# Both output projections in half blocks, the last gate group projected after the queries, and two steps a call beside the last gate block of layer one

## The chip, the core and the metric

The kernel runs on one core of a Trainium2 chip. The core has five engines with queues of their own: TensorE (PE: matmuls and transposes; PEld is its weight load), VectorE (DVE), ScalarE (ACT), GpSimd (POOL) and SyncE (SP, which here only issues transfers). Each engine works through its own list of instructions in order; between engines they wait for each other by semaphores. Matmuls write to PSUM, everything else lives in SBUF, and weights come from HBM by DMA. The metric is the time on the device in microseconds (us) of one execution; lower is better.

## The reference

Two layers over 256 tokens of width 2048, 16 heads of 128. Layer one is a gated delta rule with short convolutions, layer two is softmax attention over a band of chunks (with 256 tokens, all earlier chunks lie in it). Each has one combined input projection, a SiLU gate z that multiplies the branch, and an output projection that is added to the residual.

```python
def gated_deltanet(h, w_in, conv_w, a_log, dt_bias, out_norm_w, w_out):
    proj = h @ w_in                       # q, k, v (2048 each), z (2048), a, b (16 each)
    qkv = silu(causal_depthwise_conv(qkv, conv_w))
    ...                                   # l2-normed q, k; chunked delta rule, state between chunks
    o = rms_norm(o, out_norm_w) * silu(z)
    return o @ w_out

def chunk_band_attention(h, w_in, q_norm_w, k_norm_w, rel_bias, w_out):
    proj = h @ w_in                       # q, k, v, z (2048 each)
    q, k = rms_norm(q, q_norm_w), rms_norm(k, k_norm_w)
    ...                                   # softmax(q k / sqrt(128) + bias) @ v per head
    o = o * silu(z)
    return o @ w_out

for i in range(2):
    hn = rms_norm(h, norm_w[i])
    h = h + (gated_deltanet if i == 0 else chunk_band_attention)(hn, ...)
```

## The kernel before

**The matmuls.** All data and weights are float32. For the projections each operand is split into a high part (float32r, a cast on ACT, L195) and the rest (a subtraction on DVE, L196), and three products are summed: high x high, high x low, low x high. Weights come in chunks of 512 KB by SP, 320 of them, listed in `plan`; a chunk is two blocks of 128 input rows by 512 columns, or four by 256. Of the raw chunk there are four buffers, of each split part three, and `fetch` runs three chunks ahead (`LOOK`). So the cast and the subtraction of a chunk wait until the matmuls of an earlier chunk have let go of a buffer.

**Three forms of a projection block.** In each, one *set* of products is 128 output features x 128 input rows x 256 tokens.
- `features` (L225): 512 columns; per set three matmuls of 256 columns each (L228, L230, L231).
- `half` (L233): 256 columns; the high and the low part of the data lie side by side, so the weight's high part takes both in one matmul of 512 columns (L238), and its low part follows with one of 256 (L241): two matmuls per set. The result stands in two halves, and ACT copies one out (L304 `ev`, or L873) before DVE adds them (L305).
- `tokens` (L244): tokens on the partitions, three matmuls of 512 columns (L247 to L249).

A block accumulates over all 16 input tiles `kt` in one of two PSUM buffers `psp`; the small products of the mixers use four buffers `pss`.

**The background.** All that is not projection (convolution, delta rule, norms, attention) is written as Python generators that stand in two lists, `bgq` and `bg2`. After each pair or group of matmuls `chunk` calls `step(rate)`, which advances one generator by one piece, `rate` times. `drain()` runs everything that is left. A scheduler then orders each engine's instructions anew from data dependences, free buffers and this order as priority; the order that it leaves is the one that the engines run.

**Where the two layers end.** The output projection contracts over the heads: input tile `kt` is head `kt`'s gated output, in `gmem["h"]` and `gmem["l"]`. `ready(gmem)` steps the background until head `kt` is there. The last four heads come late, since their chain begins with the last input block. So each projection opens two blocks at once: first `kt` 0 to 11 of both (`CUT` = 6 of 8 chunks each), then `drain()`, then `kt` 12 to 15 of both. Before, those two are `features` blocks of 512 columns; four `half` blocks of 256 follow.

**The chain of the last four heads in layer one**, by lines: `v_small` transposes v on PE (L744), scales it on DVE (L746), multiplies by the inverse on PE (L753, ACT copy L755), corrects the second half on PE and DVE (L760, L763), multiplies again (L753, L755); `v_back` forms the outputs on PE (L776 to L778), squares on ACT (L779), sums on DVE (L785, L786), takes the power on POOL (L788), scales (L794); `za_small(3)` multiplies by the gate z (L710); `gated` transposes on PE (L814) and splits on ACT and DVE (L818, L819). Then `ha_small` adds the residual, which POOL's queue loads (L869), and splits it for layer two.

**The end of layer two.** For each group of four heads: keys, queries, `qk_norm`, and `attend` in four stages per head: `scores` (L1010, L1011, then DVE and exponentials on ACT, L1023), `weights` (L1031), `turned` (three transposes L1037, ACT copy L1039 `pT`), `values` (L1047, L1048). At the end of `values` DVE multiplies by the gate (L1050), ACT and DVE split (L1051, L1052). The gates z come first in layer two (four groups of 512 columns, `zb_small`: L320 scales, L935 SiLU on ACT). The tiles `ev` and `pT` share two buffers.

## Time and profile before

| what | value |
|---|---|
| time, median of 3 runs | 1024.39 us (1023.38 to 2028.42) |
| profiled execution, its own time | 1024.26 us |
| profiled execution, span first to last instruction | 1022.4 us |
| PE busy / PEld busy | 1007.9 us (99%) / 881.1 us (86%) |
| DVE busy / ACT busy / POOL busy | 694.8 us (68%) / 520.2 us (51%) / 76.3 us (7%) |
| mean granted TensorE clock | 0.997 |
| DMA | 177.55 MB, 174 GB/s |

The profiled execution takes 1.86 us more than its span, and is 0.13 us below the median. A row of the timeline gives the start and the length in us, the engine, line, operation, the tiles and shapes, how many instructions were merged, and in brackets the idle time before it with what ended it. A group of lines has the count, busy us and mean ns. Matmuls overlap, so two that follow each other are compared by their starts.

### The profile page before, as it was taken

Reading aid. Unit: us, or ns where it says so; the run is one execution under the profiler, and the core shown is the slowest. Engines: PE = TensorE matmul, PEld = TensorE weight load, DVE = VectorE, ACT = ScalarE, POOL = GpSimd, SP = SyncE. Lnnn points to the kernel's source line nnn. Section 1 sums busy time; section 2 is a strip of 40 time slices with the busy share of each in tenths; the row PEclk is TensorE's granted clock in tenths of the full one; section 3 lists DMA queues with packets and bytes.
Section 4 is the critical chain, followed back from the end, with each engine's and each line's share of the span. In section 5 each row is a group of like instructions: output and inputs, shape, how many; then the busy total and the mean of one; then the engine's idle time right before and its main releaser. Section 6 shows DMA issues by size and latency. Waiting matters only on the chain.

```text
span 1022.4 us, 15569 instructions
## 1 busy us (share of the span) xinstructions
PE 1007.9 (99%) x6094; PEld 881.1 (86%) x6094; DVE 694.8 (68%) x1111; ACT 520.2 (51%) x720; POOL 76.3 (7%) x91
## 2 busy tenths in 40 slices
PE   8999999999999999999999999999999999999998
PEld 7988788888788989899988888888888888889987
DVE  6699879998799587755766555444456666656553
ACT  7465756453646555544654444444445555555442
POOL 1004000112000000001000000000011010101000
PEclk9999999999999999999999999999999999999999
DMA  8655566555576355545856766666665555554572
GB/s 292 177 147 144 162 175 180 143 164 158 157 199 165 105 145 145 158 151 157 255 186 183 228 207 205 190 194 195 188 188 176 148 178 151 167 163 146 174 227 72
DMA packets 133736, 177.55 MB, mean 174 GB/s; under 512 B 7584, under 2 KB 89632, under 8 KB 133664
## 3 DMA queue, kind: packets, MB, share of 16 engines
q1 hardware_dynamic: 132512, 172.38, 57.1%
q0 software_dynamic: 1152, 4.19, 1.2%
q8 instruction: 47, 0.77, 0.3%
q14 instruction: 25, 0.20, 0.1%
HBM read 174.46 MB, written 2.10 MB: 173 GB/s over the span
## 4 chain that ended last, share of the span: by engine, by line
PE 95%; DVE 2%; ACT 1%; DMA 1%; issue 1%; SPq 0%; DVEq 0%; ACTq 0%
PE psp L238 27%; PE psp L241 14%; PE psp L248 11%; PE psp L249 11%; PE psp L247 11%; PE psp L231 4%; PE psp L228 4%; PE psp L230 4%; PE pss L556 2%; PE pss L753 1%; PE pss L992 1%; PE pss L1011 1%; PE pss L1047 1%; DMA wt<-in_a_w_in_dram 1%; DVE wlo L196 1%; PE pss L1037 1%
## 5 line engine op out<-in xcount | busy, mean ns | idle before, releaser
L196 DVE TENSOR_TENSOR wlo<-wt,whi 128x1024 fp32r<-128x1024 f32 (+1 forms) x321 | 392.9, 1226 | 247.2 <-ACT whi L195 238.8
L195 ACT CAST whi<-wt 128x1024 fp32r<-128x1024 f32 (+1 forms) x321 | 336.7, 1050 | 410.9 <-PE psp L238 164.0
L238 PE MATMUL psp<-xb,whi 128*128 128x512 f32 x960 | 265.7, 396 | 3.6 <-DVE ev L305 2.0
L248 PE MATMUL psp<-wlo,xb 128*128 128x512 f32 x512 | 201.1, 393 | 1.6 <-DVE wlo L196 1.6
L249 PE MATMUL psp<-whi,xb 128*128 128x512 f32 x512 | 201.5, 393 | 0.0
L247 PE MATMUL psp<-whi,xb 128*128 128x512 f32 x512 | 200.0, 391 | 0.0
L238 PEld LDWEIGHTS psp<-xb,whi 128*128 128x128 f32 x960 | 165.0, 190 | 25.9 <-DVE ev L305 2.2
L241 PEld LDWEIGHTS psp<-xb,wlo 128*128 128x128 f32 x960 | 148.4, 189 | 20.1
L241 PE MATMUL psp<-xb,wlo 128*128 128x256 f32 x960 | 157.6, 283 | 0.0
L248 PEld LDWEIGHTS psp<-wlo,xb 128*128 128x128 f32 x512 | 96.1, 188 | 21.7 <-DVE wlo L196 2.0
L247 PEld LDWEIGHTS psp<-whi,xb 128*128 128x128 f32 x512 | 96.2, 188 | 20.1 <-ACT whi L195 0.3
L249 PEld LDWEIGHTS psp<-whi,xb 128*128 128x128 f32 x512 | 96.2, 188 | 19.1
L228 PE MATMUL psp<-g,whi 128*128 128x256 f32 x256 | 73.4, 287 | 0.0
L230 PE MATMUL psp<-g,whi 128*128 128x256 f32 x256 | 73.3, 287 | 0.0
L231 PE MATMUL psp<-g,wlo 128*128 128x256 f32 x256 | 72.7, 284 | 0.0
L238 PE MATMUL psp<-g,whi 128*128 128x512 f32 x248 | 67.7, 394 | 0.0
L499 DVE SCALAR_TENSOR_TENSOR cv<-raw,sm,cv 128x254 f32<-128x254 f32 (+2 forms) x144 | 61.8, 474 | 0.1
L230 PEld LDWEIGHTS psp<-g,whi 128*128 128x128 f32 x256 | 49.1, 192 | 0.2
L228 PEld LDWEIGHTS psp<-g,whi 128*128 128x128 f32 x256 | 49.1, 192 | 0.1
L231 PEld LDWEIGHTS psp<-g,wlo 128*128 128x128 f32 x256 | 49.1, 192 | 0.1
L238 PEld LDWEIGHTS psp<-g,whi 128*128 128x128 f32 x248 | 42.4, 189 | 5.7
L241 PEld LDWEIGHTS psp<-g,wlo 128*128 128x128 f32 x248 | 38.1, 189 | 5.3
(239 smaller groups left out, 980.1 us busy)
## 6 DMA issues: line engine op xcount, KB each, us to landing
wt<-in_b_w_in_dram SPq DMA_DIRECT2D x128, 512.0 KB, 3.7
wt<-in_a_w_in_dram SPq DMA_DIRECT2D x127, 512.0 KB, 3.9
wt<-in_a_w_out_dram SPq DMA_DIRECT2D x32, 512.0 KB, 4.5
wt<-in_b_w_out_dram SPq DMA_DIRECT2D x32, 512.0 KB, 4.0
g<-in_xT_dram SPq DMA_DIRECT2D x8, 256.0 KB, 4.5
dl<-in_xT_dram POOLq DMA_DIRECT2D x4, 512.0 KB, 5.4
dl<-in_relb_dram POOLq DMA_DIRECT2D x4, 512.0 KB, 5.2
out_dram<-cv SPq DMA_DIRECT2D x2, 512.0 KB, 4.2
```

The costliest lines, as they stand in the source:

```text
L195: act.copy(out=hi[:, js], in_=wt[:, js])
L196: dve.tensor_tensor(out=lo[:, js], in0=wt[:, js], in1=hi[:, js].bitcast(F32), op=ALU.subtract)
L228: pe.matmul(ps, lhsT=hi[:, j, fs], rhs=xb[:, kt, 0, :], start=(kt == 0 and s % 2 == 0), stop=False, skip_group_check=True)
L230: pe.matmul(ps, lhsT=hi[:, j, fs], rhs=xb[:, kt, 1, :], start=False, stop=False, skip_group_check=True)
L231: pe.matmul(ps, lhsT=lo[:, j, fs], rhs=xb[:, kt, 0, :], start=False, stop=(kt == KT - 1), skip_group_check=True)
L238: pe.matmul(ps[:, s], lhsT=hi[:, j, s * P:(s + 1) * P], rhs=xb[:, ks[j], :, :], start=(ks[j] == 0), stop=False, skip_group_check=True)
L241: pe.matmul(ps[:, s, 0, :], lhsT=lo[:, j, s * P:(s + 1) * P], rhs=xb[:, ks[j], 0, :], start=False, stop=(ks[j] == KT - 1), skip_group_chec ...
L247: pe.matmul(ps, lhsT=xh, rhs=hi[:, j, :], start=(kt == 0), stop=False)
L248: pe.matmul(ps, lhsT=xh, rhs=lo[:, j, :], start=False, stop=False)
L249: pe.matmul(ps, lhsT=xl, rhs=hi[:, j, :], start=False, stop=(kt == KT - 1))
L499: dve.scalar_tensor_tensor(out=cv[:, i, s:], in0=raw[:, i, :T - s], scalar=conv_w(i0 + i, 3 - s), in1=cv[:, i, s:], op0=ALU.mult, op1=ALU.add)
L556: pe.matmul(dst, lhsT=kq[:, a, i, c:c + P], rhs=rhs, start=(n == 0), stop=(n == 2))
```

## The change

- **Both output projections are made of eight `half` blocks.** The two blocks that are opened together have 256 columns each, not 512, and are cut after `CUTH` = 3 of 4 chunks, again at `kt` 12. `ha_small` always copies `ev` on ACT first; the outputs go out in pieces of two feature tiles (`out_half`), and `out_small` is gone.
- **The last gate group of layer two** (columns 7680 to 8191 of `b_w_in`) is projected after the last queries, just ahead of the output projection. `values` of the last four heads therefore leaves the ungated result in `late` (an ACT copy), and `late_gates` multiplies and splits it once the gates are there, two heads at a time. The load of the last group of biases hangs on the first group of v in place of the last gate group.
- **`rate` is 2** in the last gate block of layer one.

```diff
-    CUT = (3 * CPB) // 4
     CUTH = (3 * CPH) // 4
-    def cut_halves(w, col):
+    def cut_halves(w, col, n=6):
...
-        return p + halves(w, col + 512, 6)
-    for c0, c1 in ((0, CUT), (CUT, CPB)):
-        for j in range(2):
-            plan += wide(a_w_out, 512 * j, c0, c1)
-    plan += halves(a_w_out, 1024, 4)
-    plan += cut_halves(b_w_in, 6144)
+        return p + halves(w, col + 512, n)
+    plan += cut_halves(a_w_out, 0)
+    plan += cut_halves(b_w_in, 6144, 4)
...
-    for c0, c1 in ((0, CUT), (CUT, CPB)):
-        for j in range(2):
-            plan += wide(b_w_out, 512 * j, c0, c1)
-    plan += halves(b_w_out, 1024, 4)
+    plan += halves(b_w_in, 7680, 2)
+    plan += cut_halves(b_w_out, 0)
...
-    bgq.append(za_small(3, block("tokens", xb)))
+    bgq.append(za_small(3, block("tokens", xb, 2)))
...
-    def ha_small(n, ps, ks):
+    def ha_small(ps, ks):
...
-        two = len(ps.shape) == 4
-        if two:
-            ev = work.tile([P, 2, T], F32, name="ev", tag="ev")
-            act.copy(out=ev, in_=ps[:, :, 1, :])
+        ev = work.tile([P, 2, T], F32, name="ev", tag="ev")
+        act.copy(out=ev, in_=ps[:, :, 1, :])
         yield 1
-        if n < 2:
-            dve.tensor_copy(out=hmem["h"][0:1, k0 + 8, 0:1], in_=ps[0:1, 0, 0:1])
-        dve.tensor_tensor(out=h, in0=ps[:, :, 0, :] if two else ps, in1=h, op=ALU.add)
-        if two:
-            dve.tensor_tensor(out=h, in0=h, in1=ev, op=ALU.add)
+        if k0 in (0, 4):
+            dve.tensor_copy(out=hmem["h"][0:1, k0 + 8, 0:1], in_=ev[0:1, 0, 0:1])
+        dve.tensor_tensor(out=h, in0=ps[:, :, 0, :], in1=h, op=ALU.add)
+        dve.tensor_tensor(out=h, in0=h, in1=ev, op=ALU.add)
...
-    pa = [acc("features") for _ in range(2)]
-    for n in (CUT, CPB - CUT):
+    pa = [acc("half") for _ in range(2)]
+    for n in (CUTH, CPH - CUTH):
         for j in range(2):
-            if n != CUT and j == 0:
+            if n != CUTH and j == 0:
                 drain()
             for _ in range(n):
-                chunk("features", pa[j], gmem["b"], 2, ready(gmem))
-            if n != CUT:
-                a_done(j, pa[j], 4 * j, 4 * j + 4)
-    for j in range(4):
-        a_done(j + 2, block("half", gmem["b"], 2), 8 + 2 * j, 10 + 2 * j)
+                chunk("half", pa[j], gmem["b"], 2, ready(gmem))
+            if n != CUTH:
+                bgq.append(ha_small(pa[j], slice(2 * j, 2 * j + 2)))
+    for j in range(2, 8):
+        bgq.append(ha_small(block("half", gmem["b"], 2), slice(2 * j, 2 * j + 2)))
...
-    for j in (1, 2, 3):
+    for j in (1, 2):
         bgq.append(zb_small(j, pair(xb)))
...
+            if gi == 3:
+                act.copy(out=late[:, i, :], in_=ps[:, :T])
+                return
...
+    late = hmem["m"][:, 8192:9216].rearrange("p (h t) -> p h t", h=4)
+    def late_gates():
+        for i in range(0, 4, 2):
+            o, hs = late[:, i:i + 2, :], slice(12 + i, 14 + i)
+            dve.tensor_tensor(out=o, in0=o, in1=bmem["z"][:, hs, :], op=ALU.mult)
+            act.copy(out=gmem["h"][:, hs, :], in_=o)
+            dve.tensor_tensor(out=gmem["l"][:, hs, :], in0=o, in1=gmem["h"][:, hs, :].bitcast(F32), op=ALU.subtract)
+            gmem["done"] = 14 + i
+            yield 1
...
+    bgq.append(zb_small(3, pair(xb)))
+    bgq.append(late_gates())
...
-    po = [acc("features") for _ in range(2)]
+    po, evs = [acc("half") for _ in range(2)], [[], []]
...
-    for n in range(4, 7):
+    for n in range(2, 7):
```

The built programs show what stands where. Up to the first row of layer one's output projection TensorE's list is the same in both. Line numbers of the changed kernel differ: there L190 and L191 are the cast and the subtraction (L195, L196 before), L233 and L236 the two matmuls of a `half` set (L238, L241), L299 and L300 the two halves of an eviction (L304, L305).

First TensorE in layer one, where the outputs of the last four heads are formed. Before, L776 to L778 are those products, and L228 to L231 the matmuls of the projection:

```order
L776 MATMUL pss<-dl 128x128
L777 MATMUL pss<-dl 128x128
L778 MATMUL pss<-dl 128x128
L230 MATMUL psp<-g,whi 128x256
L231 MATMUL psp<-g,wlo 128x256
L228 MATMUL psp<-g,whi 128x256
```

Now the same products are L771 to L773, and L809 (L814 before) are the transposes of the gated heads:

```order
L771 MATMUL pss<-dl 128x128
L772 MATMUL pss<-dl 128x128
L773 MATMUL pss<-dl 128x128
L809 MATMUL pss<-ident,dl 128x128 x8
L233 MATMUL psp<-g,whi 128x512 x4
L236 MATMUL psp<-g,wlo 128x256 x4
```

Before, projection matmuls follow the products, and the transposes come after 76 of them. Now the transposes follow directly, and the projection goes on behind them.

Next VectorE at the same place. Before, from the correction L763 on, with the subtractions of weight chunks (L196) between the links:

```order
L763 SCALAR_TENSOR_TENSOR dl<-pss,nbr,dl 128x128 x4
L196 TENSOR_TENSOR wlo<-wt,whi 128x1024 x2
L785 TENSOR_REDUCE so<-dl 128x8
L786 SCALAR_TENSOR_TENSOR so<-so,epq 128x8
L196 TENSOR_TENSOR wlo<-wt,whi 128x1024
L794 TENSOR_TENSOR dl<-pss,ro 128x2x2x128 x2
L710 TENSOR_TENSOR dl<-dl,kT 128x4x128 x2
L196 TENSOR_TENSOR wlo<-wt,whi 128x1024 x2
L819 SCALAR_TENSOR_TENSOR g<-pss,sm,g 128x2x256 x2
```

Now, where L758 is that correction, L780 to L705 are L785 to L710, L814 is L819, and L870 and L871 begin the eviction of the first half block:

```order
L191 TENSOR_TENSOR wlo<-wt,whi 128x1024 x3
L758 SCALAR_TENSOR_TENSOR dl<-pss,nbr,dl 128x128 x4
L780 TENSOR_REDUCE so<-dl 128x8
L781 SCALAR_TENSOR_TENSOR so<-so,epq 128x8
L789 TENSOR_TENSOR dl<-pss,ro 128x2x2x128 x2
L705 TENSOR_TENSOR dl<-dl,kT 128x4x128 x2
L814 SCALAR_TENSOR_TENSOR g<-pss,sm,g 128x2x256 x2
L191 TENSOR_TENSOR wlo<-wt,whi 128x1024
L870 COPY dl<-ev 1x1
L871 TENSOR_TENSOR dl<-psp,dl 128x512
```

The subtractions between the links are gone; three stand ahead of L758, and one ahead of the first eviction.

Last ScalarE at the end of layer two. Before, the last two heads' copies (L1039) and splits (L1051) stand between casts:

```order
L195 CAST whi<-wt 128x1024
L1039 COPY pT<-pss 128x384
L1051 CAST g<-gt 128x256
L195 CAST whi<-wt 128x1024
L1051 CAST g<-gt 128x256
L195 CAST whi<-wt 128x1024 x10
L304 COPY ev<-psp 128x512
```

Now L1046 is the copy into `late`, L1034 is L1039, L921 the SiLU of the last gates with a table load of its own, and L1067 the split of the late gates:

```order
L190 CAST whi<-wt 128x1024
L1046 COPY dl<-pss 128x256
L1034 COPY pT<-pss 128x384
L299 COPY ev<-psp 128x512
L1046 COPY dl<-pss 128x256
L921 ACT_TABLE_LOAD
L921 ACTIVATE tt<-tt 128x1024
L190 CAST whi<-wt 128x1024
L1067 CAST g<-dl 128x2x256 x2
```

The eviction of the last gate block (L299) stands behind the last head's `pT`, and the SiLU with its table load behind the last copy into `late`.

More of the change, by code (lines that the diff above doesn't have):

```diff
@@ L851, in tile_hybrid_trunk @@
         bgq.append(v_small(gi, ps))
-    bgq.append(za_small(3, block("tokens", xb)))
+    bgq.append(za_small(3, block("tokens", xb, 2)))
     hmem = {}
-    def ha_small(n, ps, ks):
-        if n == 0:
+    def ha_small(ps, ks):
+        if ks.start == 0:
             m = slot("dl", 48)
@@ L928, in zb_small @@
         scaled(z, evs, scales["h"][1])
-        bias, hs = bmem["bias"], slice(4 * gi, 4 * gi + 4)
-        dve.tensor_copy(out=bias[0:1, 4 * gi, 0:1], in_=z[0:1, 0, 0:1])
-        nc.gpsimd.dma_start(out=bias[:, hs, :], in_=relb[:, hs, :])
-        pool.memset(bias[0:64, hs, 192:256], NEG)
+        if gi < 3:
+            bias_load(gi, z[0:1, 0, 0:1])
         yield 1
@@ L936, in zb_small, with bias_load @@
         yield 1
+    def bias_load(gi, after):
+        bias, hs = bmem["bias"], slice(4 * gi, 4 * gi + 4)
+        dve.tensor_copy(out=bias[0:1, 4 * gi, 0:1], in_=after)
+        nc.gpsimd.dma_start(out=bias[:, hs, :], in_=relb[:, hs, :])
+        pool.memset(bias[0:64, hs, 192:256], NEG)
     while "x" not in hmem:
@@ L959, in vb_small @@
                            scale=scales["h"][0][:, t:t + 1])
+        if gi == 0:
+            bias_load(3, bmem["v"][0:1, 0, 0:1])
         yield 1
@@ L1099, in out_half @@
         yield 1
-    po = [acc("features") for _ in range(2)]
-    for n in (CUT, CPB - CUT):
+    po, evs = [acc("half") for _ in range(2)], [[], []]
+    for n in (CUTH, CPH - CUTH):
         for j in range(2):
-            if n != CUT and j == 0:
+            if n != CUTH and j == 0:
                 drain()
             for _ in range(n):
-                chunk("features", po[j], gmem["b"], 1, ready(gmem))
-            if n != CUT:
-                bgq.append(out_small(j, po[j]))
-    for n in range(4, 7):
+                chunk("half", po[j], gmem["b"], 1, ready(gmem))
+            if n != CUTH:
+                joined(po[j], evs[j])
+                bgq.append(out_half(j, evs[j]))
+    for n in range(2, 7):
         evs = []
```

8 lines of the change are left out of this document (removed).

## The prediction

> **What bounds the kernel now.** I read the page first, then the waits, then single stretches of the timeline.
>
> ```profile
> PE 1007.9 (99%) x6094; PEld 881.1 (86%) x6094; DVE 694.8 (68%) x1111; ACT 520.2 (51%) x720; POOL 76.3 (7%) x91
> PE 95%; DVE 2%; ACT 1%; DMA 1%; issue 1%; SPq 0%; DVEq 0%; ACTq 0%
> DVE wlo L196 <- ACT whi L195: 238.8, 211, 4.0
> ACT whi L195 <- PE psp L238: 164.0, 100, 4.1
> ```
>
> PE works 99% of the span and carries 95% of the chain that ended last. ACT waits for PE to free weight buffers, and DVE for ACT: the split of the weights follows PE. So only two things count: how long PE's own matmuls take, and whether PE comes to stand still. Where the projections of both layers are, it does not stand still now; the columns are the stretch, its us, busy us (instructions) of PE, PEld, DVE, ACT and POOL, granted clock, DMA share and GB/s:
>
> ```profile
> 441.20:483.50 42.30, 42.30 (x361) 42.30 (x360) 26.63 (x38) 18.89 (x23) 5.06 (x4) 1.00 0.47 149
> 483.50:540.00 56.50, 56.50 (x355) 50.84 (x354) 39.33 (x53) 32.56 (x52) 1.50 (x2) 1.00 0.70 221
> 918.00:972.00 54.00, 54.00 (x440) 53.49 (x439) 31.71 (x61) 26.22 (x46) 2.99 (x3) 1.00 0.52 164
> ```
>
> The first row is layer one's output projection up to `kt` 11, the second the rest of it, the third the end of layer two. There is no idle time to win in them: the change can win only what the other form saves, and lose cover.
>
> **The form.** Starts of matmuls, in the `features` form and in the `half` form:
>
> ```profile
> 477.68 0.28 PE L228 MATMUL psp<-g,whi 128*128 128x256 f32 x1
> 477.80 0.28 PE L230 MATMUL psp<-g,whi 128*128 128x256 f32 x1
> 477.92 0.28 PE L231 MATMUL psp<-g,wlo 128*128 128x256 f32 x1
> 478.04 0.28 PE L228 MATMUL psp<-g,whi 128*128 128x256 f32 x1
> ...
> 511.95 1.09 PE L238 MATMUL psp<-g,whi 128*128 128x512 f32 x4
> 512.88 0.63 PE L241 MATMUL psp<-g,wlo 128*128 128x256 f32 x4
> 513.35 0.86 PE L238 MATMUL psp<-g,whi 128*128 128x512 f32 x3
> ```
>
> A `features` set takes 478.04 - 477.68 = 0.36 us, four `half` sets 513.35 - 511.95 = 1.40, so 0.35 each. 256 sets change (2 projections x 2 blocks x 4 slices x 16 `kt`): 256 x 0.01 = **-2.6 us**. [...]
>
> **Layer one's end: the cover.** Before head 12 is needed, PE had 2 x 6 chunks of 8 sets, 96 x 0.36 = 34.6 us of projection; now 2 x 3 chunks, 48 x 0.35 = 16.8 us. Beside them runs the chain of the last four heads. Its links now, in the profile:
>
> ```profile
> 458.48 1.06 PE L760 MATMUL pss<-dl 128*128 128x128 f32 x8
> 458.19 1.05 ACT L195 CAST whi<-wt 128x1024 fp32r<-128x1024 f32 x1 [2.05 <-PE psp L230]
> 459.27 1.23 DVE L196 TENSOR_TENSOR wlo<-wt,whi 128x1024 fp32r<-128x1024 f32 x1 [2.54 <-ACT whi L195]
> 460.42 1.12 DVE L763 SCALAR_TENSOR_TENSOR dl<-pss,nbr,dl 128x128 f32<-128x128 f32 x4
> 464.52 0.59 ACT L755 COPY dl<-pss 128x512 f32<-128x512 f32 x1 [1.51 <-PE pss L753]
> 469.37 0.60 ACT L779 ACTIVATE dl<-pss 128x512 f32<-128x512 f32 x1 [0.30 <-PE pss L778]
> 470.00 1.22 DVE L785 TENSOR_REDUCE so<-dl 128x8 f32<-128x1024 f32 x1 [1.07 <-ACT dl L779]
> 471.56 1.64 POOL L788 TENSOR_TENSOR ro<-so,nhalf 128x8 f32<-128x8 f32 x1 [25.66 <-DVE so L786]
> 473.50 1.28 DVE L794 TENSOR_TENSOR dl<-pss,ro 128x512 f32<-128x512 f32 x2
> 474.82 1.30 DVE L710 TENSOR_TENSOR dl<-dl,kT 128x512 f32<-128x512 f32 x2
> 478.98 0.82 PE L814 MATMUL pss<-ident,dl 128*128 128x128 f32 x6
> 479.50 1.27 ACT L818 ACTIVATE g<-pss,sm 128x512 fp32r<-128x512 f32 x2 [1.41 <-PE pss L814]
> 480.22 1.41 DVE L819 SCALAR_TENSOR_TENSOR g<-pss,sm,g 128x512 fp32r<-128x512 f32 x2 [0.88 <-ACT g L818]
> ```
>
> From L760 to the first ready split the chain takes 458.48 to 480.97, and PE fills it with projection. In the order now, all 96 matmuls of the first part stand ahead of L760 (L755 there), and from it to the transposes nothing is left that PE could do: both `psp` buffers are held, and `kt` 12 waits for this very chain. Let 0 be the last projection matmul's end. L763 stands behind three subtractions, the third of a chunk whose buffer PE frees only at 0: a cast (from -0.2) 1.05 and a subtraction 1.22 give 2.1. L763 ends at 3.2, L753's last three (behind four of L776 and L777) at 4.35, L755 at 4.95. L776 to L778, eight products of two passes at 0.11, end at 6.85 and L779 at 7.5. From L785's start to L788's are 1.56: 9.05, and L788 ends at 10.7, L794 and L710 at 13.35. Two transposes and their latency: 13.75; one L818: 14.45; one L819: **15.2**. In it PE does L760, L753, L776 to L778, 20 products x 0.22, and 8 transposes x 0.11, together 5.3 us. It stands for **9.9 us**, where it stood 0. From below: 8.5 if L763 needn't wait for the buffer. From above: 11.5, with 0.1 us more at each of 16 handovers.
>
> **Then the first eviction.** The next block needs a PSUM buffer of the two. Both blocks now end 1.4 us apart, and the first is freed by a cast, the copy `ev`, a subtraction, the 1x1 copy and the add:
>
> ```profile
> L873 ACT COPY ev<-psp 128x512 f32<-128x512 f32 x4 | 2.3, 577 | 0.0
> L877 DVE COPY dl<-psp 1x1 f32<-1x1 f32 x2 | 0.3, 148 | 1.3 <-PE psp L231 1.3
> L305 DVE TENSOR_TENSOR ev<-psp,ev 128x512 f32<-128x512 f32 x33 | 22.5, 681 | 0.0
> 480.43 1.80 POOL L869 DMA_DIRECT2D dl<-in_xT_dram  x2 [7.23 <-ACT g L818]
> DMA to landing us min/median/max: 4.3/5.4/6.6
> ```
>
> From the first block's end: -0.2 + 1.05 (cast), then the subtraction 1.22 on DVE beside `ev` 0.58 on ACT, then 0.15 + 0.68: 2.9. PE is done with the second block at 1.4 and waits **1.5 us** (0 would need the eviction not to stand behind that cast and subtraction; 3 if the residual comes 1.5 late). The residual's load on POOL's queue is issued with L818 as before, at about 14.5 + 0.3, and lands 5.4 later, at 20.2; the add is due at 15.2 + 4.2 + 2.2 = 21.6. The latest landing, 6.6, still fits.
>
> **The clock.** Where PE stood for 2.0 us, the next stretch ran at half the clock; where it stood for 1.6 it did not:
>
> ```profile
> 115.11:118.52 3.41, 1.39 (x8) 1.00 0.72 191
> 118.53:121.93 3.40, 3.40 (x12) 0.50 0.43 135
> 50.20:53.60 3.40, 1.79 (x12) 1.00 0.21 74
> 118.04 0.85 PE L238 MATMUL psp<-xb,whi 128*128 128x512 f32 x2 [2.02 <-DVE ev L305]
> ```
>
> In the chain, PE has nothing from 6.85 to about 12.8, 6 us on end. So the clock falls to a half, and comes back after a stretch of 3.4 us of work: **+1.7 us**; 0 if it stays up as after the 1.6 us, 3.4 if two such stretches follow. [...]
>
> **Layer two's end.** The gates moved behind the queries are 128 matmuls (64 sets, 22.4 us) moved, not added: no cost. They cover the norm of the last queries and the first scores. The first part of the output projection is again 16.8 us, and the last head's order is tight:
>
> ```profile
> L1039 ACT COPY pT<-pss 128x384 f32<-128x384 f32 x16 | 7.7, 479 | 16.8 <-PE pss L1037 16.8
> L1051 ACT CAST g<-gt 128x256 fp32r<-128x256 f32 x16 | 6.5, 406 | 1.4 <-DVE gt L1050 1.4
> L1023 ACT ACT_TABLE_LOAD x1 | 1.3, 1283 | 0.0
> L935 ACT ACTIVATE tt<-tt 128x1024 f32<-128x1024 f32 x4 | 4.2, 1056 | 0.0
> ```
>
> The last two heads' `values` and the last `turned` stand back to back on PE: the last `values` waits for `pT`, 0.16 + 0.48 + 0.1 = 0.75. Then the second block needs the gates' PSUM buffer, freed by L304 (0.58, right behind `pT`) and L305 (0.68), some 0.55 after `values`: together **+1.3 us** (0 to 3.6, the upper end if the next cover fails). That cover: from L305 PE has 24 sets, 8.4 us. Beside them ACT copies (0.41), loads the table (1.28), does the SiLU (1.06); DVE multiplies (0.69); ACT casts a chunk and splits (1.05 + 0.58); DVE subtracts a chunk and splits (1.2 + 0.7): about 6.1 of them, 2.3 to spare.
>
> **Edits at nothing.** Two steps a call beside the last gate block: up to the projection TensorE's order is the same, so nothing moves. The bias load on another link: it has the k and q blocks of three groups to land. The stores on SP's queue, four small in place of two, stand among loads that run three chunks ahead. The extra evictions (four `ev` of 0.58 and four adds of 0.69 a projection) lie on engines that are busy 51% and 68%; uncovered, 5 us a projection.
>
> **Sum.** -2.6 + 9.9 + 1.5 + 1.7 + 1.3 = +11.8 us on the profiled execution's 1024.26 (1.86 beyond its span, 0.13 below the median): **1036 us**, 1.2% slower, which a bound of 2% (about what a measurement of this kernel can tell) calls the same.
>
> **Rivals.** *Cover enough*: the chain stays hidden, only the form counts: 1024.3 - 2.6 = 1021.7. For it: the chain's links need 15 us and the cover is 16.8. Against: all 96 matmuls stand ahead of L760, none beside the links. Chance 0.07. *Idle without the clock*: the stall comes, but the small products within it keep the clock up: 1036.1 - 1.7 = 1034.4. For it: PE does 5.3 us of them in the 15. Against: 6 us on end is more than the 2.0 that sufficed. 0.13. *Clock lost for long*, slower than before by over 2%: the stall's half clock lasts until the projection's later blocks. Over 1044.9 it takes 1044.9 - 1034.4 = 10.5 us lost, so 21 us at half, over six stretches; seven would give 1046.3. Against: 118.53 shows one stretch and then full. 0.04. *The change does nothing*, because the scheduler fills the gap: 1024; the order speaks against it, 0.02.
>
> **Numbers.** The forecast has 0.74. The low ends add up to 1024.3 - 2.6 + 8.5 = 1030, the high ends to 1024.3 - 2.6 + 11.5 + 3 + 3.4 + 3.6 = 1043; not all come together, so 1030 to 1042, which takes in the second rival. Under 1003.9 (faster): 0.01, since 20 us are nowhere to win. Over 1044.9: 0.05, the clock and what the chain may hide. The rest, 0.94, is the same.
>
> **What would show it.** Right: PE idle near 463 to 478 us of some 10 us in three gaps, the longest about 6 ahead of the transposes; L788 between them; a stretch at 0.50 behind; a gap at the next block with the add as releaser; two gaps under 1 us near 957. Wrong: PE busy throughout there, or gaps elsewhere. The forecast fails if projection matmuls run inside the chain, or if the SiLU's chain at the end takes over 8.4 us.

## The result, and the profile after

The changed kernel takes **1037.31 us** (median; 1032.49 to 1037.59), **1.0132 times** the kernel before, with a 95% interval of 1.0114 to 1.0149: a slowdown of 1.3%. (Of the kernel before, two executions of 2028 and 1240 us were disturbed and are left out; in the experiments its executions lie between 1019.56 and 1026.06.) The profiled execution took 1037.59 us, its span is 1035.9 us, 13.5 us longer than before.

The page of the changed kernel, busy time and the chain that ended last:

```profile
PE 1011.3 (98%) x5838; PEld 870.6 (84%) x5838; DVE 700.4 (68%) x1119; ACT 526.1 (51%) x731; POOL 76.5 (7%) x91
PE 94%; DVE 2%; ACT 1%; issue 1%; DMA 0%; SPq 0%; POOL 0%; DVEq 0%; ACTq 0%; POOLq 0%
```

PE is the bound as before, and 256 matmuls fewer did not make this kernel faster. Where the 13.5 us are is read from stretches (columns as in the prediction: the stretch, its us, busy us of PE, PEld, DVE, ACT and POOL, granted clock, DMA share, GB/s). First the kernel before: layer one's output projection, from its first matmul to the first of layer two, and all that follows:

```profile
441.10:540.01 98.91, 98.91 (x713) 93.24 (x712) 65.96 (x91) 51.57 (x75) 6.55 (x6) 1.00 0.60 190
540.01:1022.37 482.36, 477.50 (x2562) 412.51 (x2560) 269.82 (x385) 225.83 (x307) 27.09 (x36) 1.00 0.59 178
```

The changed kernel: the same two stretches, and within the first one the part from the end of the last projection matmul that needs no late head to the first one that does:

```profile
461.36:477.36 16.00, 7.14 (x49) 5.85 (x47) 7.04 (x14) 3.72 (x6) 1.92 (x2) 0.88 0.21 66
...
441.74:553.34 111.60, 101.47 (x586) 88.40 (x584) 68.89 (x97) 53.51 (x79) 6.57 (x6) 0.97 0.52 168
553.34:1035.89 482.55, 476.90 (x2434) 405.80 (x2432) 272.75 (x387) 230.05 (x314) 27.26 (x36) 1.00 0.59 178
```

Layer one's output projection went from 98.91 to 111.60 us, **+12.69**; all that follows from 482.36 to 482.55, **+0.19**; ahead of it 441.74 - 441.10 = +0.64. Before, PE did not stand still in it; now it is idle for 111.60 - 101.47 = 10.1 us: 16.00 - 7.14 = 8.9 us while the chain of the last four heads runs, and 1.26 us at the first eviction. TensorE's timeline there (start, us, line, count, idle time before it and what ended that):

```profile
463.55 0.49 PE L748 MATMUL pss<-dl,tt 128*128 128x128 f32 x2 [1.30 <-DVE dl L758]
466.27 0.49 PE L773 MATMUL pss<-dl 128*128 128x128 f32 x2 [0.68 <-ACT dl L750]
474.30 2.14 PE L809 MATMUL pss<-ident,dl 128*128 128x128 f32 x8 [5.97 <-DVE dl L705]
477.36 2.08 PE L233 MATMUL psp<-g,whi 128*128 128x512 f32 x4 [0.92 <-DVE g L814]
...
481.69 1.08 PE L233 MATMUL psp<-g,whi 128*128 128x512 f32 x4
483.08 1.09 PE L233 MATMUL psp<-g,whi 128*128 128x512 f32 x4
485.91 1.16 PE L233 MATMUL psp<-g,whi 128*128 128x512 f32 x4 [1.26 <-ACT ev L866]
```

The chain of the last four heads, on VectorE, ScalarE and GpSimd in that order (the lines are five lower than in the kernel before: L780 is its L785, L783 its L788, L789 its L794, L705 its L710):

```profile
463.15 1.12 DVE L758 SCALAR_TENSOR_TENSOR dl<-pss,nbr,dl 128x128 f32<-128x128 f32 x4
468.99 1.22 DVE L780 TENSOR_REDUCE so<-dl 128x8 f32<-128x1024 f32 x1 [4.72 <-ACT dl L774]
472.23 1.29 DVE L789 TENSOR_TENSOR dl<-pss,ro 128x512 f32<-128x512 f32 x2 [1.81 <-POOL ro L783]
473.55 1.29 DVE L705 TENSOR_TENSOR dl<-dl,kT 128x512 f32<-128x512 f32 x2
468.36 0.60 ACT L774 ACTIVATE dl<-pss 128x512 f32<-128x512 f32 x1 [0.29 <-PE pss L773]
470.56 1.64 POOL L783 TENSOR_TENSOR ro<-so,nhalf 128x8 f32<-128x8 f32 x1 [24.01 <-DVE so L781]
```

From the products' squares (468.36) over sum, power and two multiplications to 473.55 + 0.65 (the first of the two L705) each link begins within 0.15 us of the end of the one before. Nothing else is on these engines in that time, and PE waits for the end of it. The clock around it, in stretches of 3.41 us:

```profile
466.84:470.26 3.42, 1.49 (x14) 1.29 (x12) 1.23 (x2) 1.20 (x2) 0.00 (x0) 1.00 0.00 0
470.26:473.67 3.41, 0.00 (x0) 0.00 (x0) 1.56 (x4) 0.00 (x0) 1.64 (x1) 1.00 0.01 2
473.67:477.08 3.41, 2.14 (x8) 1.43 (x8) 1.70 (x3) 1.25 (x2) 0.00 (x1) 0.50 0.00 0
477.08:480.49 3.41, 3.13 (x9) 2.67 (x10) 0.88 (x2) 0.08 (x1) 1.78 (x2) 0.50 0.49 121
480.50:483.91 3.41, 3.41 (x20) 2.96 (x19) 0.03 (x1) 1.10 (x2) 0.00 (x0) 1.00 0.53 185
```

Two stretches at 0.50, not one: the first holds the transposes, the second the first sets. Layer two's end, TensorE and then the gates' last split on VectorE:

```profile
947.75 0.70 PE L1042 MATMUL pss<-pT,kT 128*128 128x256 f32 x2 [0.62 <-ACT pT L1034]
948.97 1.21 PE L233 MATMUL psp<-g,whi 128*128 128x512 f32 x4 [0.29 <-DVE ev L300]
953.84 1.29 DVE L1068 TENSOR_TENSOR g<-dl,g 128x512 fp32r<-128x512 f32 x2
```

### The profile page after: what moved, and what is told of

It reads as the page before. It is cut to its first block, busy times and chain, and to the rows that moved or that the text cites. A ratio compares the mean times of both kernels' runs of the same rounds, so it can differ in the third digit from the quotient of the medians.

```text
span 1035.9 us, 15092 instructions
## 1 busy us (share of the span) xinstructions
PE 1011.3 (98%) x5838; PEld 870.6 (84%) x5838; DVE 700.4 (68%) x1119; ACT 526.1 (51%) x731; POOL 76.5 (7%) x91
## 4 chain that ended last, share of the span: by engine, by line
PE 94%; DVE 2%; ACT 1%; issue 1%; DMA 0%; SPq 0%; POOL 0%; DVEq 0%; ACTq 0%; POOLq 0%
PE psp L233 32%; PE psp L236 16%; PE psp L243 11%; PE psp L242 11%; PE psp L244 11%; PE pss L551 2%; PE pss L748 1%; PE pss L987 1%; PE psp L226 1%; PE pss L1006 1%; PE psp L225 1%; PE psp L223 1%; DVE wlo L191 1%; PE pss L1042 1%; DMA g<-in_xT_dram 0%
## 5 line engine op out<-in xcount | busy, mean ns | idle before, releaser
L191 DVE TENSOR_TENSOR wlo<-wt,whi 128x1024 fp32r<-128x1024 f32 (+1 forms) x321 | 393.0, 1226 | 253.6 <-ACT whi L190 244.0
L190 ACT CAST whi<-wt 128x1024 fp32r<-128x1024 f32 (+1 forms) x321 | 336.6, 1050 | 407.9 <-PE psp L233 197.7
L233 PE MATMUL psp<-xb,whi 128*128 128x512 f32 x960 | 266.7, 397 | 3.6 <-DVE ev L300 2.0
L233 PEld LDWEIGHTS psp<-xb,whi 128*128 128x128 f32 x960 | 165.8, 190 | 26.1 <-DVE ev L300 2.2
L236 PEld LDWEIGHTS psp<-xb,wlo 128*128 128x128 f32 x960 | 149.3, 190 | 20.3
L236 PE MATMUL psp<-xb,wlo 128*128 128x256 f32 x960 | 159.1, 284 | 0.0
L233 PE MATMUL psp<-g,whi 128*128 128x512 f32 x504 | 139.4, 398 | 2.5 <-ACT ev L866 1.3
L233 PEld LDWEIGHTS psp<-g,whi 128*128 128x128 f32 x504 | 86.9, 190 | 14.9 <-ACT ev L866 1.4
L236 PEld LDWEIGHTS psp<-g,wlo 128*128 128x128 f32 x504 | 77.6, 190 | 10.7
L236 PE MATMUL psp<-g,wlo 128*128 128x256 f32 x504 | 80.8, 282 | 0.0
L970 POOL TENSOR_SCALAR ssn<-ssn,uh 128x4 f32<-128x4 f32 x16 | 9.2, 591 | 241.1 <-DVE ssn L968 241.1
L300 DVE TENSOR_TENSOR ev<-psp,ev 128x512 f32<-128x512 f32 x37 | 25.2, 681 | 0.2 <-ACT ev L299 0.2
L492 ACT ACTIVATE cv<-raw,sm 128x256 f32<-128x256 f32 x48 | 21.6, 501 | 7.2 <-DVE raw L315 5.9
L299 ACT COPY ev<-psp 128x512 f32<-128x512 f32 x37 | 21.5, 580 | 1.4 <-PE psp L236 1.4
L226 PE MATMUL psp<-xb,wlo 128*128 128x256 f32 x64 | 18.3, 286 | 1.0 <-DVE wlo L191 1.0
```

The costliest lines, as they stand in the source:

```text
L190: act.copy(out=hi[:, js], in_=wt[:, js])
L191: dve.tensor_tensor(out=lo[:, js], in0=wt[:, js], in1=hi[:, js].bitcast(F32), op=ALU.subtract)
L226: pe.matmul(ps, lhsT=lo[:, j, fs], rhs=xb[:, kt, 0, :], start=False, stop=(kt == KT - 1), skip_group_check=True)
L233: pe.matmul(ps[:, s], lhsT=hi[:, j, s * P:(s + 1) * P], rhs=xb[:, ks[j], :, :], start=(ks[j] == 0), stop=False, skip_group_check=True)
L236: pe.matmul(ps[:, s, 0, :], lhsT=lo[:, j, s * P:(s + 1) * P], rhs=xb[:, ks[j], 0, :], start=False, stop=(ks[j] == KT - 1), skip_group_chec ...
L299: act.copy(out=ev, in_=ps[:, :, 1, :])
```

## The experiments

The theory is that of the prediction: layer one's half blocks open only half as many columns ahead of the last four heads, so their chain lies open. The rivals are that the loss sits in layer two, that it comes from the half form's own evictions and buffers, and, for one term of it, that the clock plays no part. All results, with the stage of layer one's output projection (first matmul to layer two's first), the time in it that PE is not busy, and how long the clock stood at a half in it:

| kernel | median us | ratio to before (95%) | stage us | PE idle us | half clock us |
|---|---|---|---|---|---|
| before | 1022.89 | 1 | 98.91 | 0 | 0 |
| changed | 1037.31 | 1.0132 (1.0114 to 1.0149) | 111.60 | 10.1 | 6.83 |
| layer one alone | 1035.92 | 1.0133 (1.0108 to 1.0157) | 112.04 | 10.1 | 10.24 |
| layer two alone | 1022.07 | 0.9997 (0.9984 to 1.0011) | 98.92 | 0 | 0 |
| changed, chain longer | 1039.95 | 1.0177 (1.0151 to 1.0204) | 117.56 | 15.2 | 17.07 |
| before, chain longer | 1027.86 | 1.0065 (1.0041 to 1.0089) | 104.69 | 3.5 | 3.41 |
| changed, chain shorter | 1030.28 | 1.0084 (1.0051 to 1.0117) | 107.70 | 5.8 | 6.83 |
| half of the cover back | 1029.19 | 1.0059 (1.0037 to 1.0080) | 106.13 | 4.2 | 6.83 |
| filled, first try | 1037.06 | 1.0135 (1.0115 to 1.0156) | 114.15 | 5.9 | 6.83 |
| filled, second try | 1037.02 | 1.0154 (1.0128 to 1.0181) | 114.15 | 5.1 | 0 |
| filled, third try | 1033.21 | 1.0106 (1.0085 to 1.0127) | 109.83 | 5.5 | 0 |
| layer two alone, other buffers | 1021.51 | 0.9986 (0.9973 to 0.9999) | 98.92 | 0 | 0 |

(The median of before is that of the first group of experiments; the others had 1021.97 and 1022.53 beside them, and each ratio is to its own, that of the changed kernel to two executions of 1023.38 and 1024.39 us. Stage, idle time and clock are read from one profiled execution of each kernel.)

One part of the change can be settled from the built programs alone: with one step a call instead of two in the last gate block, every engine's order in the built program is the same row for row, so that edit cannot have moved the time.

**Where: each layer alone.** Layer one alone keeps the change's edits to layer one and undoes those to layer two; layer two alone is the reverse:

```diff
 # layer two alone: layer one's projection as before
-    plan += cut_halves(a_w_out, 0)
+    for c0, c1 in ((0, CUT), (CUT, CPB)):
+        for j in range(2):
+            plan += wide(a_w_out, 512 * j, c0, c1)
+    plan += halves(a_w_out, 1024, 4)
...
-    pa = [acc("half") for _ in range(2)]
+    pa = [acc("features") for _ in range(2)]
```

Expected of layer one alone:

> Layer one as in the changed kernel (its whole output projection in half blocks, two steps a call beside the last gate block and these), layer two as in the kernel before. Theory (cover): the half blocks of layer one hold only 256 columns per accumulator, so the sets that need no late head last 16.8 us instead of 34.6 us, less than the chain of the last four heads; the changed kernel's output-projection stage of layer one grew from 98.91 to 111.60 us, and all of that must be here: stage 110.5 to 112.5 us, time 12 to 13 us above the kernel before, 1035.5 to 1037.5 us. Rival (the loss comes from the order of weights and gates in layer two, and the stage in the trace only shows it early): under 1028 us, with a stage under 103 us.

Expected of layer two alone:

> Layer one as in the kernel before, layer two as in the changed kernel (output projection in half blocks, the last gates projected behind the last queries). Theory (cover): 128 sets in half form save 1.3 us, the two gaps ahead of the output projection (0.62 and 0.29 us in the changed kernel's trace) and smaller ones give it back: 1023.0 to 1025.0 us, a stage of layer one of 98.5 to 99.5 us. Rival (layer two's late gates cost several us that the ledger of the stages put elsewhere): 1027 us or more.

Layer one alone has the whole loss, 1.0133, layer two alone none of it, 0.9997. The stage of layer one, in the one and in the other kernel:

```profile
436.57:548.61 112.04, 101.91 (x585) 88.73 (x584) 68.91 (x97) 53.52 (x79) 6.57 (x6) 0.95 0.52 167
```

```profile
438.04:536.96 98.92, 98.92 (x714) 93.25 (x712) 65.97 (x91) 51.60 (x75) 6.56 (x6) 1.00 0.60 190
```

So the rival that puts it in layer two falls. Layer two's edits are worth nothing that can be measured either way, although there, too, half blocks replace two blocks of the other form; its median, 1022.07 us, is 0.9 us under the 1023.0 to 1025.0 expected, with the stage as expected. Layer one alone runs the same instructions in this stage as the changed kernel, with the same waits of 5.97, 0.92 and 1.26 us. It had three stretches at half clock in it (10.24 us), not two, and the stage is 0.44 us longer.

**Why: the chain made longer and shorter.** In the changed kernel, and in the kernel before, four more sums of squares in the chain of the last four heads; and in the changed kernel that chain without its norm:

```diff
 # longer (both kernels)
-        dve.reduce_sum(out=so, in_=sq, axis=AX.X)
+        for _ in range(5 if gi == 3 else 1):
+            dve.reduce_sum(out=so, in_=sq, axis=AX.X)
 # shorter (changed kernel; squares left out in the same way)
+        if gi < 3:
             dve.reduce_sum(out=so, in_=sq, axis=AX.X)
             ...
+        else:
+            ro = beta[:, h0:h0 + 4, :]
```

Expected of the changed kernel with the longer chain:

> The changed kernel with the sums of squares of the last four heads made five times instead of once (four more VectorE instructions of 1.22 us, 4.9 us, in the chain from the products to the power). Theory (that chain is what TensorE stands for, with nothing beside it): the idle time of 5.97 us ahead of the transposes becomes 10.7 to 11.0 us, the stage of layer one's output projection 116.3 to 117.0 us (111.60 plus 4.9), up to 1.7 us more if another stretch of 3.41 us falls to half clock; time 1041.5 to 1044 us. Rival (TensorE stands for something else, the evictions or the split of the weights, and the chain ends in its shadow): stage within 1 us of 111.60.

Expected of the kernel before with the longer chain:

> The kernel before with the same four more instructions of 1.22 us in the chain of the last four heads. Its transposes stand in TensorE's queue 2.2 us behind the end of what they wait for (476.12 to 478.28 us). Theory (34.6 us of sets that need no late head cover the chain with 2 to 2.5 us to spare): of 4.9 us the cover takes 2.2 and 2.7 us show, plus up to 1.7 us if the idle time costs a stretch of the clock; stage of layer one's output projection 98.92 plus 2.4 to 4.5 us, time 2 to 5 us above the kernel before. Rival one (the chain has far more cover than 2.5 us, since the order is made anew around it): no change, under 0.5 us. Rival two (no cover at all, as in the changed kernel): plus 4.9 us or more.

Expected of the shorter chain:

> The changed kernel without the norm of the last four heads: their squares, the sums, the constant and the power are left out and a tensor that is there already scales them, so those heads are not normed. It takes the steps from 468.2 to 472.2 us out of the chain (squares, 1.22 us sum, 0.17 us constant, 1.64 us power). Theory (chain without cover): the idle time of 5.97 us becomes 2.0 to 2.3 us, the stage of layer one's output projection 107.4 to 108.2 us with both stretches at half clock left, 105.7 to 106.5 us if one of them goes; time 1031 to 1034 us. Rival (something else ends at the same time): stage within 1 us of 111.60.

TensorE's first transposes in the changed kernel with the longer chain, then with the shorter one:

```profile
475.51 2.14 PE L810 MATMUL pss<-ident,dl 128*128 128x128 f32 x8 [10.98 <-DVE dl L705]
```

```profile
466.41 0.44 PE L813 MATMUL pss<-ident,dl 128*128 128x128 f32 x2 [1.51 <-DVE dl L705]
467.01 1.39 PE L813 MATMUL pss<-ident,dl 128*128 128x128 f32 x6 [0.16 <-DVE dl L705]
```

5.97 us of idle time became 10.98, so 4.9 us more in the chain showed as 5.0, in full; the stage grew by 5.96, with the clock at a half for 17.07 us in place of 6.83. The shorter chain took 5.97 to 1.67 (2.0 to 2.3 expected), and the stage fell by 3.90, with some 4.0 us taken out of the chain. So in this stage of the changed kernel a microsecond of the chain is about a microsecond of time. The whole kernel moves with it, by the ratios +4.6 us (1.0177 against 1.0132) and -4.9 us (1.0084); both medians, 1039.95 and 1030.28 us, lie under the ranges expected, by 1.6 and 0.7 us.

In the kernel before the same edit cost 5.8 us of the stage, more than the 2.4 to 4.5 expected, and the reason is one that the expectation had wrong. TensorE and VectorE there:

```profile
481.52 0.44 PE L815 MATMUL pss<-ident,dl 128*128 128x128 f32 x2 [2.88 <-DVE dl L710]
483.44 0.80 PE L228 MATMUL psp<-g,whi 128*128 128x256 f32 x2 [0.45 <-ACT g L819]
```

```profile
465.76 2.47 DVE L786 TENSOR_REDUCE so<-dl 128x8 f32<-128x1024 f32 x2 [1.07 <-ACT dl L779]
468.15 1.22 DVE L196 TENSOR_TENSOR wlo<-wt,whi 128x1024 fp32r<-128x1024 f32 x1
469.28 1.21 DVE L786 TENSOR_REDUCE so<-dl 128x8 f32<-128x1024 f32 x1
...
472.15 2.47 DVE L786 TENSOR_REDUCE so<-dl 128x8 f32<-128x1024 f32 x2
...
480.78 1.28 DVE L710 TENSOR_TENSOR dl<-dl,kT 128x512 f32<-128x512 f32 x2
```

Where projection runs beside the chain, VectorE also splits its weights, and the scheduler put those subtractions between the sums. From the first sum's start to L710's end it took 482.06 - 465.76 = 16.3 us, where it took 476.12 - 470.00 = 6.1 before. Of 10.2 us more, PE stood for 3.5 (104.69 us of stage, 101.20 busy), mostly the 2.88 and 0.45 above, and one stretch of 3.41 us at half clock came with it. So the 34.6 us of cover took up 6.7 of the 10.2 us, and then they came to an end. By the stage alone rival two (no cover, 4.9 us or more) would fit as well; it falls because without cover all of the 10.2 us would have stood open. What 4.9 us alone would have cost the run cannot say, because it did not add only those.

**How much cover: half of it given back.** The first of the two blocks takes 512 columns in the old form, the second stays a half block:

```diff
-    plan += cut_halves(a_w_out, 0)
+    for c0, c1, h0, h1 in ((0, (3 * CPB) // 4, 0, CUTH), ((3 * CPB) // 4, CPB, CUTH, CPH)):
+        plan += wide(a_w_out, 0, c0, c1)
+        plan += half(a_w_out, 512, h0, h1)
+    plan += halves(a_w_out, 768, 5)
...
-    pa = [acc("half") for _ in range(2)]
+    kinds = ("features", "half")
+    pa = [acc(k) for k in kinds]
```

> The changed kernel, but of the two blocks of layer one's output projection that are begun ahead of the last four heads the first takes 512 columns in the other form (four accumulators of 256 each, as before), the second 256 in half form. So the sets that need no late head last 17.3 + 8.4 = 25.7 us, half way between 34.6 us (kernel before) and 16.8 us (changed kernel). First ready sets came 40.5 us after the stage's first matmul in the kernel before and 35.6 us after it in the changed one; half way, 38 us, less 25.7 us of sets and some 9 us of the chain's own matmuls leaves 3 us. Theory (cover): TensorE stands 2 to 5 us in place of 9.9 us, stage 101 to 105.5 us, time 3 to 6.5 us above the kernel before. Rival one (the loss comes with the half form's evictions and buffers, of which 7 of 8 are still there): stage 109 to 112 us. Rival two (25.7 us are cover enough): stage 98 to 100.5 us.

TensorE's first transposes there, and the two stretches of the clock behind them:

```profile
475.59 2.14 PE L812 MATMUL pss<-ident,dl 128*128 128x128 f32 x8 [3.85 <-DVE dl L708]
```

```profile
475.54:478.95 3.41, 3.02 (x10) 2.01 (x11) 1.70 (x3) 1.33 (x2) 0.57 (x1) 0.50 0.26 88
478.96:482.37 3.41, 3.41 (x17) 3.41 (x17) 0.30 (x1) 0.00 (x0) 1.20 (x2) 0.50 0.66 173
```

PE is idle for 4.2 us, within 2 to 5. The stage is 0.6 us over the range given, with two stretches at half in it, for which the range left too little room; the time is 6.7 us above the kernel before, 0.2 over. With 34.6, 25.7 and 16.8 us of sets that need no late head, PE is idle for 0, 4.2 and 10.1 us. Seven of eight half blocks are left in this kernel and less than half of the idle time: the rival that blames the half form's evictions for the bulk of the loss falls. Their part is the wait of 1.26 us at the first eviction, which is gone in this kernel too; the other 4.7 us of the difference lie in the chain.

**The clock: TensorE kept busy in the gap.** Matmuls whose result nothing reads, between the last products and the transposes. This is the third try; the second has 45 in place of 22, the first 60 with `ones_r` as both operands:

```diff
+        if gi == 3:
+            ps = ps_small()
+            for _ in range(22):
+                pe.matmul(ps[:, :P], lhsT=vs[:, 3, 1, :], rhs=sq[:, 3, 1, :], start=True, stop=True)
```

First try:

> The changed kernel with 60 matrix products of 128x128 more, whose result nothing reads, in TensorE's queue between the last four heads' products and the transposes that wait for their power: they lie in the idle time of 5.97 us and end before it does if one takes under 0.1 us. Theory (the idle time halves the granted clock for two stretches of 3.41 us, of which the matmuls behind the wait use about 3.1 us at half speed): no stretch at half clock near 474 us, the stage of layer one 1.4 to 1.8 us shorter than 111.60 us, time 1035.3 to 1036.2 us. Rival one (the clock's stretch costs nothing, for what is behind it waits for VectorE and ScalarE anyhow): stage within 0.4 us of 111.60. Rival two (the products delay the transposes, since they run at half speed themselves): stage longer by up to 3 us.

```profile
463.28 3.10 PE L781 MATMUL pss<-ones_r 128*128 128x128 f32 x26
466.22 0.44 PE L773 MATMUL pss<-dl 128*128 128x128 f32 x2
...
474.28 1.88 PE L814 MATMUL pss<-ident,dl 128*128 128x128 f32 x8 [2.32 <-DVE dl L705]
```

It said nothing on the clock: depending on no late data, 26 of the 60 went ahead of the chain's own last products (L773) and held the chain up, the second rival's loss by another way. So the next try's operand was the last square.

> The changed kernel with 45 more matrix products of 128x128, whose result nothing reads and whose operand is the last square of the last four heads, so that they cannot stand ahead of the products of these heads as they did in the first try: they begin at about 469 us and, at 0.11 us each, end by 474 us, ahead of the transposes. They leave the chain alone. Theory (the idle time takes the clock down): no stretch at half clock at 474 us, the stage of layer one's output projection 109.5 to 110.3 us (111.60 less 1.3 to 2.0), time 1035 to 1036 us. Rival one (the clock falls all the same, since about 1 us of idle time is left on either side of them, or since such products do not count as work): stage within 0.4 us of 111.60. Rival two (the first try's loss of 2.5 us comes from the products themselves and not from their place): stage 113 us or more.

```profile
467.56 10.31 PE L781 MATMUL pss<-dl 128*128 128x128 f32 x90 [0.69 <-ACT dl L774]
477.71 1.04 PE L814 MATMUL pss<-ident,dl 128*128 128x128 f32 x8
479.87 1.20 PE L233 MATMUL psp<-g,whi 128*128 128x512 f32 x4 [1.13 <-DVE g L819]
```

These operands make two records a product (90 for 45), 0.226 us in place of 0.11 (26 took the 2.94 us from 463.28 to 466.22 in the first try), so the fill ran 4.9 us past the chain's end, and the stage, 114.15 us in place of 109.5 to 110.3, says nothing on the clock's price. But the clock stayed at full (granted 1.00 over the stage): eight transposes took 1.04 us, not 2.14, and the first four sets' wide matmuls 1.20, not 2.08. With half as many:

> As the second try, with 22 products in place of 45. In that try 45 took 10.2 us (0.226 us each, each is two records), ended 4.9 us behind the point where the transposes could have begun, and the stage was 114.15 us; the clock stayed at full. 22 take 5.0 us and end when the transposes can begin. Theory (the idle time takes the clock down, at a price): no stretch at half clock near 474 us, and the stage 114.15 less 4.9, 109.0 to 109.8 us, so the clock's price is 1.8 to 2.6 us; time 1034.5 to 1036 us. Rival (the clock costs nothing, the second try's number is only by chance so): stage 111.2 to 112 us.

```profile
465.38 5.18 PE L781 MATMUL pss<-dl 128*128 128x128 f32 x44 [0.69 <-ACT dl L774]
470.75 1.38 PE L814 MATMUL pss<-ident,dl 128*128 128x128 f32 x8 [0.20 <-DVE dl L705]
473.38 1.21 PE L233 MATMUL psp<-g,whi 128*128 128x512 f32 x4 [1.24 <-DVE g L819]
```

The stage is 109.83 us, 1.77 us under the changed kernel's: that is what the clock cost there, and the rival (111.2 to 112) falls. It is one execution against one: against layer one alone, the same instructions with three stretches at half, it would be 2.2 us. The chain's own length is as it was, 470.75 - 438.10 = 32.65 us from the stage's first matmul to the transposes, against 474.30 - 441.74 = 32.56, so the other 11 us (109.83 - 98.91) remain, and the kernel is still 1.0106 times the kernel before. Its median, 1033.21 us, is 1.3 us under the range expected.

**A version to keep.** Layer two as changed, layer one as before, and the last gates' evictions in the buffers of the queries' squares, which frees them from the two `ev` buffers:

```diff
-            ev = work.tile([P, 2, T], F32, name="ev", tag="ev")
+            ev = wk("cv")[:, 0:2] if late else work.tile([P, 2, T], F32, name="ev", tag="ev")
...
-    bgq.append(zb_small(3, pair(xb)))
+    bgq.append(zb_small(3, pair(xb, late=True)))
```

> The kernel with layer two alone changed, and in addition the evictions of the last gate block write into another set of buffers (those of the squares of the queries), so that they no longer wait for the buffers of the block before. The places of the attention's steps move with it by up to one block. Theory (the two gaps ahead of layer two's output projection, 0.62 and 0.29 us, hang on ScalarE's and VectorE's order around these evictions): 0.5 to 1.2 us under the kernel with layer two alone changed, 1022.3 to 1024.0 us. Rival (the gaps hang on the last probabilities alone, whatever the evictions do): equal to it within 0.3 us.

The two gaps of 0.62 and 0.29 us are gone, and one of 1.12 stands a block later:

```profile
946.95 1.19 PE L237 MATMUL psp<-g,whi 128*128 128x512 f32 x4 [1.12 <-DVE ev L304]
```

So the idle time moved, and the step that I expected did not happen. The median is 0.56 us under that of layer two alone, within the 0.5 to 1.2 expected, but the executions of each kernel spread over 3.6 and 4.4 us. At 0.9986 (0.9973 to 0.9999) it is the fastest kernel measured, by an interval that barely leaves out 1, and it is not told apart from layer two alone.

## Why the prediction was right, and where not

- **The time, and the step that failed.** 1036.1 us was forecast within 1030 to 1042; 1037.31 came. The mechanism and its place were right: the cover is too short, and PE stands for the chain. The step that failed is the last one of the sum, from +11.8 us, "1.2% slower", to "the same", by way of "a bound of 2% (about what a measurement of this kernel can tell)". The measurement tells far less than 2%: the interval, 1.0114 to 1.0149, is 0.35% wide. So the 1.2% of the sum was itself a slowdown that can be measured, and 1.3% was measured; the 0.94 on "the same" holds only as a statement about the 2% line. Among the terms of the sum it was the clock's that failed; see below.
- **The form, -1.3 us a layer.** Four `half` sets take 483.08 - 481.69 = 1.39 us in the changed kernel, as read before, so the rows' price holds. But the saving could not be seen by itself: in layer two PE was busy for only 0.60 us less (476.90 in place of 477.50) and idle for 0.79 us more. Where the rest of the 1.3 us went there is open.
- **The cover, +9.9 us.** From the last projection matmul that needs no late head to the first that does, 15.2 us were worked out; it took 16.00. Less the same 5.3 us of PE's own work that is 10.7, where 9.9 was forecast. (The profile itself counts 7.14 us of PE as busy there and 8.9 as idle, since the transposes took 2.14 us at half clock, where 0.9 was counted, and since a row counts as busy to its end: L771's from 463.87 is 0.39 us long, and the next starts at 464.10.) The links up to the end of L710 (L705 now) were 13.35; the trace has 473.55 + 1.29 - 461.36 = 13.5. The excess comes behind, 2.5 us in place of 1.85: eight transposes at half clock take 2.14 us, where the second filled kernel shows 1.04 at full clock. The lower bound's reason (L758 might not have to wait for a chunk) did not hold: it ends at 464.27, 2.9 after the last matmul, 3.2 forecast.
- **First eviction, +1.5.** 485.91 - 483.08 less 1.39 is +1.4. The trace names the copy `ev` of the second block as the releaser and not the add; the two end within 0.1 us, and in the kernel with the longer chain it names the add, so which of them ended it is open. The load of the residual held nothing up.
- **The clock, +1.7: the term that was mis-sized.** The step was that the clock "comes back after a stretch of 3.4 us of work". The stretch from 118.53 that this was read from had PE busy for all of its 3.40 us; the one behind this gap was filled with 2.14 us of transposes and 1.27 us of idle time, and the clock stayed down for a second one, 6.83 us in all. On the sets this cost 481.69 - 477.36 less 2 x 1.40, so 1.5 us, and on the transposes another 1.1 us, which the chain's term holds: 2.6 us in place of 1.7. Taking the clock's fall away (third filled kernel) brought back 1.8: from the transposes' start to the first set it took 473.38 - 470.75 = 2.63 us there, in place of 477.36 - 474.30 = 3.06, so of the 1.1 us only 0.4 came through. So that the size came out near is luck, by two errors: one stretch too few, and part of its price hidden.
- **Layer one in sum.** -1.3 + 10.7 + 1.4 + 1.5 = +12.3 by the rows, +12.69 measured, +11.8 forecast; 0.4 us are not assigned.
- **Layer two's end, +1.3 against the form's -1.3.** Measured +0.19 in all. The two gaps are there with their releasers, 0.62 and 0.29 us (0.75 and 0.55 forecast), at 948 us and not near 957, so 0.9 in place of 1.3; with the form's -1.3 that leaves 0.6 us not assigned. The late gates' chain ends at 953.84 + 1.29 = 955.13; 24 sets from 948.97 last until 957.49, so 2.4 us are to spare (2.3 forecast).
- **Ahead of the stage.** The prediction had nothing there, since TensorE's order is the same up to it; +0.64 us came. The trace of the changed kernel has three stretches of 3.41 us at half clock ahead of the stage (from 50.42, 118.69 and 265.46), that of the kernel before two (from 12.72 and 118.53).
- **The rivals.** *Cover enough* and *the change does nothing* fall with 10.1 us of idle time in the stage. *Idle without the clock* falls with the two stretches at 0.50; its time, 1034.4, is near what the third fill gave, 1033.2, where the clock was kept up by other means (1.00 over the stage). *Clock lost for long* falls with full clock from 480.50 on.

## What to carry to other kernels

A buffer's worth of accumulation that waits for a late operand is cover, and cover is columns per buffer times the part of the contraction that is ready: a form that is 3% faster per set but holds half the columns lost 18 us of it, and with it ten times what it saved. Before a form is changed at a hand-over, add up the chain that must hide there from its own rows, link by link, and set the new cover against it; in layer two, where the moved gates were ready 2.4 us before they were needed, the same form cost nothing that could be measured. And a filler that must not be in the way has to depend on the data behind which it belongs.

## What the runs showed of the hardware

In the traces of the two kernels the granted clock is 1.00 or 0.50, and it stood at 0.50 for 3.41 us at a time, or once for 6.83 (from 473.67 above). In the kernel before it fell behind the stretch from 115.11, which has 2.02 us of idle time on PE; in the changed kernel it fell behind the stretch from 470.26, which is all idle, and stayed at 1.00 behind the one from 466.84, with 1.93. The same 1.6 us of idle time near 50 us of the program was followed by a stretch at half in the changed kernel, shown here, and by none in the kernel before (the prediction's stretch from 50.20):

```profile
47.00:50.42 3.42, 1.82 (x13) 1.44 (x12) 2.80 (x4) 2.31 (x5) 0.00 (x0) 1.00 0.42 137
50.42:53.83 3.41, 3.41 (x13) 2.93 (x12) 3.41 (x11) 1.00 (x3) 0.00 (x0) 0.50 0.58 149
```

So in these two traces the idle time of a stretch does not settle by itself what the clock does behind it, and no run shows what else does. The same wait lies in a stretch from 47.00 in the one execution and from 50.20 in the other; as an estimate from half of 3.41 us, such waits can move the time by up to 1.7 us each with no change in the program. That would fit the +0.64 us ahead of the stage, and that executions of the kernel before differ by some 6 us; neither was tested by itself.

Nor did every stretch at half bring the clock back. Behind the stretch from 118.53 in the kernel before, without idle time, and the one from 477.08 in the changed kernel, with 3.41 - 3.13 = 0.28 us of it, the clock was at 1.00 again. Behind the one from 473.67, with 1.27 us, it was still at 0.50, and so it was in the kernel with half of the cover behind the stretch from 475.54, in which PE was busy for 3.02 of 3.41 us and idle for 0.39. Which part of such a stretch decides it was not tested.
